# A four-layer encoder on one core: the layer norm's subtraction of the mean on VectorE instead of GpSimd

## The chip, the core and the metric

The kernel runs on one core of one Trainium2 chip. A core has five engines with a queue of instructions each: TensorE (PE: matmuls, and PEld, the weight loads), VectorE (DVE), ScalarE (ACT), GpSimd (POOL) and SyncE (SP, which issues most of the transfers here). An engine works through its queue in order; an instruction may wait for semaphores that other engines raise. The metric is the device time of one execution in microseconds (us), of which the median over several runs counts.

## What is computed

Sixteen meta tokens and 256 input tokens, 2048 wide, go through four layers. Each has an input projection, attention (neighbourhood attention in layers 1 and 4, differential attention in layer 2, a sliding window in layer 3), a gate, an output projection, and a layer norm of the scaled input plus the output. Cut to what matters here:

```python
def _layer_norm(x, g, b):
    xf = x.astype(F32)
    mu = jnp.mean(xf, -1, keepdims=True)
    var = jnp.mean(jnp.square(xf - mu), -1, keepdims=True)
    y = (xf - mu) * lax.rsqrt(var + LN_EPS) * g.astype(F32) + b.astype(F32)
    return y.astype(x.dtype)

for i in range(DEPTH):                       # 4 layers: kinds A, B, C, A
    y = branch_of_kind(h, w_in, ...)         # projection, attention, gate
    out = jnp.einsum('ble,ed->bld', y, w_out[i])
    h = _layer_norm(DEEPNORM_ALPHA * h + out, ln_g[i], ln_b[i])
```

## The kernel before

Activations lie transposed: the 2048 features as 16 tiles `d0` to `d15` of 128 partitions, the 272 tokens along the free axis. Every product is made of three matmuls in fp32r, with both operands split into a high and a low half: `mm3` issues high by high (L160), high by low (L161) and low by high (L162).

**Weights.** They arrive in chunks of 1 MB (`raw`, three buffers, issued on SP at L218). A chunk holds four granules; a granule is 128x512 weights, four k-tiles of one output tile, and feeds 12 matmuls. `split_to` splits each granule eight granules ahead of its use: ScalarE casts the high half `wh` (L168), VectorE subtracts it from `raw` to get the low half `wl` (L169). There are 9 buffers of each half. An output tile of a projection is 4 granules, 48 matmuls, collected in one of three PSUM banks `acc`.

**Between two layers.** When the last output tile of a layer is done, `norm_stats` sums over the features with four small matmuls (L795, L796) and VectorE and ScalarE make `negmu`, the negative mean (L802), and `rstd` (L803 to L809, where L809, kept as `self.newton`, is the last). In the meantime TensorE goes on: the first seven output tiles of the next layer (`deferred`) are multiplied with activations that have the factor g but neither mean nor deviation yet, called `h` or `y` in the rows. `rows` corrects their results afterwards: VectorE takes off the mean (L331), GpSimd multiplies by the deviation (L334, and L333 for the bias of a query tile).

**`normalise`** makes the true activations for the tiles from the eighth on. For each of the 16 tiles: GpSimd adds `negmu` to `d` (L825), VectorE multiplies by g and `rstd` (L827), ScalarE adds b and rounds to the high half (L830), VectorE makes the low half (L831). L827 may not stand ahead of L809 in VectorE's queue (`issue_after`); L825 has no such bound. This happens three times, ahead of layers 2, 3 and 4; the last norm has a function of its own, `norm_last`, in which VectorE does part of the additions (L848).

**What sets the order.** The four kinds of work (matmuls, splits, norm, attention tasks) are written in one program, and a scheduler orders the instructions of each engine when the kernel is built, by times that it estimates. The order is then fixed for the run.

In attention, `tr` are transposes (L484, L492, L629 to L631, L683), `sc` the scores, `nm` their row maxima (L533, L661), `vs` a value tile and `v_mid` a copy of its meta columns that GpSimd makes (L399, L401).

Of the kernel before, what the change touches and what calls it, by code (L numbers as in the profile page):

```python
# [14 lines left out]
ALU = mybir.AluOpType  # L15
# [89 lines left out]
def whole(t):  # L105
    return t.rearrange("p a b -> p (a b)")[:, :NTOK]
# [14 lines left out]
class Emit:  # L121
# [695 lines left out]
    def normalise(self, l):  # L817

        nc = self.nc
        negmu, rstd, _ = yield from self.need(("stats", l - 1), 0)  # L820
        self.nh, self.nl = [None] * KT, [None] * KT
        for k in range(KT):
            g, b = self.lnp[:, l - 1, k, 0:1], self.lnp[:, l - 1, k, 1:2]
            t = whole(self.d[k])
            nc.gpsimd.tensor_tensor(out=t, in0=t, in1=whole(negmu), op=ALU.add)  # L825
            with self.tc.issue_after(self.newton.ins):
                nc.vector.scalar_tensor_tensor(out=t, in0=t, scalar=g, in1=whole(rstd), op0=ALU.mult, op1=ALU.mult)  # L827
            yield
            self.nh[k], self.nl[k], _ = self.pair(l % 2, k)
            nc.scalar.activation(whole(self.nh[k]), t, AF.Identity, bias=b)  # L830
            nc.vector.scalar_tensor_tensor(out=whole(self.nl[k]), in0=t, scalar=b, in1=whole(self.nh[k]).bitcast(F32),  # L831
                                           op0=ALU.add, op1=ALU.subtract)
        self.done(("normalised", l))
# [172 lines left out]
```

## Time and profile before

| | |
|---|---|
| median of 3 runs | 1998.03 us (1996.39 to 1998.17) |
| profiled execution, its own time | 1996.35 us |
| its span, first to last instruction | 1994.5 us |
| TensorE busy | 1958.0 us, 98% of the span |
| VectorE busy | 1448.7 us, 73% |
| ScalarE busy | 1100.3 us, 55% |
| GpSimd busy | 495.8 us, 25% |
| granted TensorE clock, mean | 0.996 of full |

Busy time is a mean over the span. Whether an engine limits a stretch is read from that stretch: which engine has no gap there, and who waits for whom. The three norms between layers lie at about 540, 1075 and 1461 us after the span's start.

### The profile page before, as it was taken

To read this page: it belongs to the slowest core of one execution; us is meant where nothing else is said; L and a number is where in the kernel's file an instruction comes from. 1 tells how busy PE (TensorE), PEld (TensorE's weight loads), DVE (VectorE), ACT (ScalarE), POOL (GpSimd) and SP (SyncE) were. 2 spreads that over 40 slices of the span, in tenths; PEclk is the share of its full clock that TensorE was granted. 3 is DMA by queue.
4 is the path that set the end of the run, shared out by engine and by line. 5 is a ranking of instruction groups with operands and counts; after the bars stand their busy time and mean duration, and the time that the engine had idled before them with its cause. 6 is when DMAs were issued, how large, how long until landed. Compare 5 with 4: busy or idle time off the path is not lost.

```text
span 1994.5 us, 40444 instructions
## 1 busy us (share of the span) xinstructions
PE 1958.0 (98%) x15794; PEld 1948.4 (98%) x15794; DVE 1448.7 (73%) x2642; ACT 1100.3 (55%) x2381; POOL 495.8 (25%) x735
## 2 busy tenths in 40 slices
PE   9999999999999999999999999999999999999995
PEld 9999999999999999999999999999999999999995
DVE  6666666668798677767798987777988666666685
ACT  6555554554566555555555655565565555555553
POOL 1100011124443122112354332223542001110053
PEclk9999999999999999999999999999999999999998
DMA  8444444444454444444453444444435444444441
GB/s 277 170 162 166 167 160 169 156 164 154 154 185 149 150 168 149 162 162 149 149 188 128 170 148 149 149 152 174 169 128 202 160 173 175 166 168 174 168 174 61
DMA packets 53039, 323.97 MB, mean 162 GB/s; under 512 B 6256, under 2 KB 12528, under 8 KB 15344
## 3 DMA queue, kind: packets, MB, share of 16 engines
q1 hardware_dynamic: 51984, 320.76, 45.6%
q8 instruction: 124, 2.03, 0.4%
q10 hardware_dynamic: 864, 0.63, 0.1%
q14 instruction: 67, 0.55, 0.1%
HBM read 319.27 MB, written 2.10 MB: 161 GB/s over the span
## 4 chain that ended last, share of the span: by engine, by line
PE 92%; DVE 5%; issue 1%; DMA 1%; POOL 1%; ACT 0%; DVEq 0%; SPq 0%; ACTq 0%; POOLq 0%
PE acc L160 28%; PE acc L162 28%; PE acc L161 28%; DVE wl L169 2%; DVE d L827 1%; PE sc L162 1%; PE sc L161 1%; PE sc L160 1%; PE o L161 1%; PE o L162 1%; PE o L160 1%; PE tr L484 1%; PE tr L492 1%; POOL ht L334 0%; DMA raw<-in_wts 0%
## 5 line engine op out<-in xcount | busy, mean ns | idle before, releaser
L169 DVE TENSOR_TENSOR wl<-raw,wh 128x512 fp32r<-128x512 f32 x1184 | 865.8, 738 | 413.3 <-ACT wh L168 401.9
L168 ACT CAST wh<-raw 128x512 fp32r<-128x512 f32 x1184 | 724.0, 618 | 662.9 <-PE acc L161 631.6
L160 PE MATMUL acc<-y,wh 128*128 128x272 f32 (+2 forms) x2448 | 706.5, 289 | 0.0
L161 PE MATMUL acc<-y,wh 128*128 128x272 f32 (+2 forms) x2448 | 704.4, 288 | 0.0
L162 PE MATMUL acc<-y,wl 128*128 128x272 f32 (+2 forms) x2448 | 701.2, 286 | 2.1 <-DVE wl L169 2.1
L162 PE MATMUL acc<-h,wl 128*128 128x272 f32 (+3 forms) x2288 | 662.3, 290 | 4.9 <-DVE wl L169 4.7
L160 PE MATMUL acc<-h,wh 128*128 128x272 f32 (+3 forms) x2288 | 661.8, 290 | 1.4 <-ACT wh L168 1.3
L161 PE MATMUL acc<-h,wh 128*128 128x272 f32 (+3 forms) x2288 | 660.3, 289 | 0.0
L162 PEld LDWEIGHTS acc<-y,wl 128*128 128x128 f32 x2448 | 461.4, 188 | 3.3 <-DVE wl L169 3.2
L161 PEld LDWEIGHTS acc<-y,wh 128*128 128x128 f32 x2448 | 461.4, 188 | 0.0
L160 PEld LDWEIGHTS acc<-y,wh 128*128 128x128 f32 x2448 | 461.0, 188 | 0.4
L162 PEld LDWEIGHTS acc<-h,wl 128*128 128x128 f32 x2288 | 431.6, 189 | 7.8 <-DVE wl L169 7.5
L160 PEld LDWEIGHTS acc<-h,wh 128*128 128x128 f32 x2288 | 432.1, 189 | 2.3 <-ACT wh L168 1.9
L161 PEld LDWEIGHTS acc<-h,wh 128*128 128x128 f32 x2288 | 431.4, 189 | 0.0
L366 DVE RECIPROCAL ez<-ez 128x272 f32<-128x272 f32 (+1 forms) x64 | 116.8, 1825 | 25.3 <-POOL ez L364 25.3
L367 POOL TENSOR_TENSOR gate<-gate,ez 128x272 f32<-128x272 f32 (+1 forms) x64 | 65.6, 1026 | 112.3 <-DVE ez L366 112.2
L774 POOL TENSOR_TENSOR os<-os,d 128x272 f32<-128x272 f32 (+1 forms) x56 | 63.2, 1128 | 111.2 <-DVE d L724 69.8
L364 POOL TENSOR_SCALAR ez<-ez 128x272 f32<-128x272 f32 (+1 forms) x64 | 27.8, 434 | 197.6 <-ACT ez L363 197.4
L427 POOL MEMSET vs<- 128x16 f32 x32 | 3.6, 112 | 233.1 <-PE tr L492 194.6
L775 POOL TENSOR_TENSOR os<-os,sq 128x272 f32<-128x272 f32 (+1 forms) x56 | 54.5, 973 | 2.6 <-DVE wl L169 2.5
L825 POOL TENSOR_TENSOR d<-d,negmu 128x272 f32<-128x272 f32 x48 | 47.4, 1024 | 22.9 <-DVE negmu L802 22.9
L439 POOL MEMSET s<- 128x16 f32 x32 | 3.6, 113 | 174.0 <-PE tr L489 167.0
(271 smaller groups left out, 1915.9 us busy)
## 6 DMA issues: line engine op xcount, KB each, us to landing
raw<-in_wts SPq DMA_DIRECT2D x293, 1024.0 KB, 4.8
bias<-in_bias_a SPq DMA_DIRECT2D x32, 184.0 KB, 2.3
raw<-in_wts SPq DMA_DIRECT2D x12, 256.0 KB, 5.0
d<-in_xT SPq DMA_DIRECT2D x16, 136.0 KB, 4.5
out_h<-raw SPq DMA_DIRECT2D x8, 256.0 KB, 2.2
dist<-in_dist_b ACTq DMA_DIRECT2D x1, 272.0 KB, 5.2
dist<-in_dist_c ACTq DMA_DIRECT2D x1, 272.0 KB, 5.7
lnp<-in_lnp ACTq DMA_DIRECT2D x1, 64.0 KB, 2.6
```

Of the source, the lines that this page charges most:

```text
L160: mm(out, lhsT=lh, rhs=rh, start=start, stop=False)
L161: mm(out, lhsT=lh, rhs=rl, start=False, stop=False)
L162: mm(out, lhsT=ll, rhs=rh, start=False, stop=stop)
L168: nc.scalar.copy(out=hi, in_=src)
L169: nc.vector.tensor_sub(out=lo, in0=src, in1=hi.bitcast(F32))
L364: nc.gpsimd.tensor_scalar(out=view(ez), in0=view(ez), scalar1=1.0, scalar2=1.0, op0=ALU.mult, op1=ALU.add)
L366: nc.vector.reciprocal(view(ez), view(ez))
L367: nc.gpsimd.tensor_tensor(out=view(zc), in0=view(zc), in1=view(ez), op=ALU.mult)
L484: nc.tensor.transpose(tr[:96, at[c]:at[c] + 128], s[:, c // 2, c % 2 * 96:c % 2 * 96 + 96], ident)
L774: eng.tensor_tensor(out=view(self.s1), in0=view(self.s1), in1=d, op=ALU.add)
L775: eng.tensor_tensor(out=view(self.s2), in0=view(self.s2), in1=sq, op=ALU.add)
L825: nc.gpsimd.tensor_tensor(out=t, in0=t, in1=whole(negmu), op=ALU.add)
```

## The change

The 48 additions of `negmu` (16 at each of three norms) move from GpSimd to VectorE, and into the block that keeps them behind L809 in VectorE's queue. The operation, its operands and its results are the same. Everything else in the text is unchanged; the line of the addition becomes L826.

```diff
         for k in range(KT):
             g, b = self.lnp[:, l - 1, k, 0:1], self.lnp[:, l - 1, k, 1:2]
             t = whole(self.d[k])
-            nc.gpsimd.tensor_tensor(out=t, in0=t, in1=whole(negmu), op=ALU.add)
             with self.tc.issue_after(self.newton.ins):
+                nc.vector.tensor_tensor(out=t, in0=t, in1=whole(negmu), op=ALU.add)
                 nc.vector.scalar_tensor_tensor(out=t, in0=t, scalar=g, in1=whole(rstd), op0=ALU.mult, op1=ALU.mult)
             yield
             self.nh[k], self.nl[k], _ = self.pair(l % 2, k)
```

The built order changes with it. Counted by line and engine, nothing else is added or dropped. The places that differ lie in three stretches behind the three norms, of some 900, 740 and 590 rows of TensorE's queue; the rest stands as before. A `+` is a row of the changed kernel's queue, a `-` one of the kernel before, a row without either stands in both. The numbers behind a name tell buffers apart.

VectorE, at the first norm, from the end of the statistics on:

```order
 L808 SCALAR_TENSOR_TENSOR rst_1285_7077<-rsx_1284_7076,rst_1285_7077 128x272
 L809 SCALAR_TENSOR_TENSOR rstd_1282_7074<-rst_1285_7077,rstd_1282_7074 128x272
+L826 TENSOR_TENSOR d0_3_73<-d0_3_73,negmu_1281_7073 128x272
 L169 TENSOR_TENSOR wl_1287_7090<-raw_1243_6849,wh_1286_7089 128x512
+L826 TENSOR_TENSOR d1_4_74<-d1_4_74,negmu_1281_7073 128x272
 L169 TENSOR_TENSOR wl_1291_7112<-raw_1255_6926,wh_1290_7111 128x512
+L826 TENSOR_TENSOR d2_5_75<-d2_5_75,negmu_1281_7073 128x272
+L826 TENSOR_TENSOR d3_6_76<-d3_6_76,negmu_1281_7073 128x272
+L826 TENSOR_TENSOR d4_7_77<-d4_7_77,negmu_1281_7073 128x272
+L169 TENSOR_TENSOR wl_1295_7135<-raw_1255_6926,wh_1294_7134 128x512
```

The additions stand between the low halves of the weights: the third of these, `wl_1295`, has five of them in front, where three L827 stood before.

TensorE, in the third output tile behind the first norm (`acc_7273`); `acc_7362` and `acc_7449` are the fourth and the fifth:

```order
 L160 MATMUL acc_7273<-h_1188_6512,wh_7155 128x274
 L161 MATMUL acc_7273<-h_1188_6512,wh_7155 128x274
+L160 MATMUL acc_7362<-h_1136_6185,wh_7198 128x274
+L161 MATMUL acc_7362<-h_1136_6185,wh_7198 128x274
+L160 MATMUL acc_7449<-h_1136_6185,wh_7291 128x274
+L161 MATMUL acc_7449<-h_1136_6185,wh_7291 128x274
 L162 MATMUL acc_7273<-h_1188_6512,wl_7156 128x274
```

The first two matmuls of later tiles, which need a high half only, now stand ahead of a matmul that needs the low half `wl_7156`.

GpSimd, some 50 us behind the second norm, where `v_mid_2800` is the copy that the transpose L631 of the second value tile reads:

```order
 L334 TENSOR_TENSOR ht_2757_14860<-ht_2757_14860,rstdq_2667_14347 128x272
-L334 TENSOR_TENSOR ht_2774_14938<-ht_2774_14938,rstd_2666_14346 128x272
-L364 TENSOR_SCALAR ez_2791_15011<-ez_2791_15011 128x272
 L399 MEMSET v_mid_2800_15060 128x96
 L401 COPY v_mid_2800_15060<-vs_2786_15001 128x3x16
+L334 TENSOR_TENSOR ht_2774_14938<-ht_2774_14938,rstd_2666_14346 128x272
+L399 MEMSET v_mid_3038_16260 128x96
+L364 TENSOR_SCALAR ez_2791_15011<-ez_2791_15011 128x272
```

The copy moves ahead of a product (L334) and of a step of the gate (L364).

## Rows read from the trace of the kernel before

**Rows 1.** The page's first part: engine, busy us, share, instructions.

```profile
PE 1958.0 (98%) x15794; PEld 1948.4 (98%) x15794; DVE 1448.7 (73%) x2642; ACT 1100.3 (55%) x2381; POOL 495.8 (25%) x735
```

**Rows 2.** Stretches: from:to us, length, busy us by engine, clock, DMA share, GB/s.

```profile
16.00:540.00 524.00, 524.00 (x4234) 523.69 (x4234) 351.21 (x651) 276.44 (x590) 85.42 (x129) 1.00 0.49 174
540.00:600.00 60.00, 56.67 (x437) 55.21 (x436) 56.80 (x90) 39.62 (x87) 28.87 (x30) 1.00 0.45 158
```

**Rows 3.** TensorE's waits: what <- for whom: us in total, times, longest.

```profile
PE acc L162 <- DVE wl L169: 6.8, 15, 1.4
PE tr L631 <- POOL v_mid L401: 2.3, 1, 2.3
...
PE sc L160 <- DVE nm L533: 1.3, 1, 1.3
...
PE tr L484 <- DVE s L470: 0.7, 1, 0.7
```

**Rows 4.** TensorE's timeline: start us, us, what; in brackets idle time before it.

```profile
540.27 0.28 PE L160 MATMUL acc<-h,wh 128*128 128x274 f32 x1
...
544.85 0.29 PE L160 MATMUL acc<-h,wh 128*128 128x274 f32 x1
...
551.09 0.29 PE L161 MATMUL acc<-h,wh 128*128 128x274 f32 x1
551.49 0.39 PE L162 MATMUL acc<-h,wl 128*128 128x274 f32 x1
...
596.14 0.30 PE L160 MATMUL sc<-kh,qh 128*16 128x272 f32 x1 [1.29 <-DVE nm L533]
...
1074.68 0.29 PE L160 MATMUL acc<-y,wh 128*128 128x274 f32 x1
...
1123.83 0.28 PE L629 MATMUL tr<-ident,vs 128*128 128x128 f32 x1
...
1459.99 0.29 PE L160 MATMUL acc<-h,wh 128*128 128x260 f32 x1
...
1460.60 0.29 PE L162 MATMUL acc<-h,wl 128*128 128x260 f32 x1
...
1461.23 0.29 PE L160 MATMUL acc<-h,wh 128*128 128x260 f32 x1
...
1510.31 0.25 PE L160 MATMUL sc<-kh,qh 128*128 128x192 f32 x1
```

**Rows 5.** VectorE's timeline at the first norm: start us, us, what.

```profile
542.65 0.58 DVE L807 SCALAR_TENSOR_TENSOR rst<-rstd 128x272 f32<-128x272 f32 x1 [0.96 <-ACT rstd L806]
...
544.19 0.90 DVE L809 SCALAR_TENSOR_TENSOR rstd<-rst,rstd 128x272 f32<-128x272 f32 x1
545.02 2.44 DVE L169 TENSOR_TENSOR wl<-raw,wh 128x512 fp32r<-128x512 f32 x2
...
550.18 1.26 DVE L169 TENSOR_TENSOR wl<-raw,wh 128x512 fp32r<-128x512 f32 x1
551.36 1.00 DVE L827 SCALAR_TENSOR_TENSOR d<-d,lnp,rstd 128x272 f32<-128x272 f32 x1
...
557.69 0.49 DVE L827 SCALAR_TENSOR_TENSOR d<-d,lnp,rstd 128x272 f32<-128x272 f32 x1
558.10 0.68 DVE L169 TENSOR_TENSOR wl<-raw,wh 128x512 fp32r<-128x512 f32 x1
558.70 0.49 DVE L831 SCALAR_TENSOR_TENSOR y<-d,lnp,y 128x272 fp32r<-128x272 f32 x1
559.11 0.49 DVE L827 SCALAR_TENSOR_TENSOR d<-d,lnp,rstd 128x272 f32<-128x272 f32 x1
```

**Rows 6.** GpSimd's timeline at the first norm: sixteen additions in a row.

```profile
541.42 15.80 POOL L825 TENSOR_TENSOR d<-d,negmu 128x272 f32<-128x272 f32 x16 [7.75 <-DVE negmu L802]
```

**Rows 7.** A group by line and shape: count, busy us, mean ns, idle before.

```profile
L774 DVE TENSOR_TENSOR os<-os,d 128x272 f32<-128x272 f32 x3 | 1.3, 443 | 0.3
```

**Rows 8.** Weight transfers: issues, KB each, median us from issue to landing.

```profile
raw<-in_wts SPq DMA_DIRECT2D x293, 1024.0 KB, 4.8
```

## The prediction

> **What bounds the kernel now.** I read the engines' busy shares first. TensorE is busy 98% of the span [rows 1], so time can only be won where it stands still. The stretches show where: between 16 and 540 us it is busy 524.00 of 524 us, around the first norm 56.67 of 60 [rows 2]. Its waits say for whom: 6.8 us in 15 waits for the low halves of weights that VectorE makes, all but 0.2 of it behind the three norms, then 2.3 us once for a GpSimd copy and 1.3 us once for a score maximum [rows 3].
>
> These figures understate the loss, since the matmuls overlap in the rows. So I count places. Thirty-six matmuls of 274 columns take 544.85 - 540.27 = 4.58 us, 0.1273 each [rows 4]. At the first norm, 402 matmuls stand in the order between the one that starts at 540.27 and the score matmul at 596.14. At full pace that is 51.2 us and would end at 591.4: 4.7 us are lost, 1.3 of them in that score's own wait, so 3.4 to the low halves. At the second norm, 360 matmuls lie between 1074.68 and 1123.83: 45.8 us at full pace, 3.3 lost. At the third, 360 lie between 1461.23 and 1510.31; 192 of them have 256 or 260 columns, at 0.61/5 = 0.122 us [rows 4]: 192 x 0.122 + 168 x 0.1273 = 44.8, 4.3 lost. **Sum: 11.0 us** lost to late low halves, at three places.
>
> Why are they late? VectorE's timeline [rows 5] gives 1.2 us for one L169 and 1.00 for one L827 until 557, and from 557.69 on 0.49 and 0.68. GpSimd's sixteen additions run from 541.42 to 557.22 without a gap [rows 6]. Both engines slow down together: an addition takes 15.80/16 = 0.99 us, and VectorE's instructions with two operands in SBUF take about twice their time beside them. The chain L807 to L809, which nothing but the norm uses, is hit as well: 0.58, 0.90, 0.90 us. TensorE runs into it at 551.09: its next matmul needs the third low half behind L809, which ends at 551.44, and starts at 551.49 instead of 551.22 [rows 4, 5].
>
> **The change part by part.** *Removed:* 16 GpSimd additions per norm, 15.8 us of a queue that nobody waits for directly except L827. Their going is worth what they cost VectorE. From 542.65 to 557.69, 15.0 us, VectorE starts the last three statistics, six L169 and six L827. At the later pace, by starts, a 272-column instruction takes 0.41 us (558.70 to 559.11) and an L169 0.60 (558.10 to 558.70) [rows 5]: 9 x 0.41 + 6 x 0.60 = 7.3 us. So the additions cost VectorE 7.7 us per norm now.
>
> *Added:* 16 additions on VectorE. No such row of L826 exists; L774, the same shape and operands on VectorE, has 443 ns [rows 7], which I take as 0.41 from start to start like its neighbours. 16 x 0.41 = 6.6 us. Bounds: 0.41 with no one else on the port, 0.92 (1.00 less the overlap) if something still slows it. I take 0.41, since GpSimd has nothing else in its queue there until the L334 of the first corrected tile.
>
> So VectorE's load per norm is nearly the same: 7.7 off, 6.6 on. What decides is **when** the low halves come. I walk through VectorE's new order behind the first norm. L809 ends at 542.65 + 3 x 0.41 = 543.9, 1.1 us earlier than now. The third low half has five additions and two low halves in front: 5 x 0.41 + 3 x 0.60 = 3.85, done at 547.7; TensorE needs it at 551.2, and one more every 12 x 0.1273 = 1.53 us. The fourth has six more small instructions in front: 550.8 against 552.7. The tightest is the fourteenth: 14 x 0.60 + 35 x 0.41 = 22.75 us, at 566.7 against 551.2 + 11 x 1.53 = 568.0, early by 1.3 us. If L807 to L809 won nothing, it would still be early by 0.2. Behind it stand seven low halves with few small instructions between, and the lead grows to 5 us. The other two norms have the same order up to a few rows; at the third, tiles of 260 columns bring the need of the fourteenth forward by up to 0.6 us, and 0.7 remain. So TensorE's waits for low halves go: **-11.0 us**.
>
> *What is late next?* The additions push back the last activations: their low halves end, by the same sum, at 582.7. TensorE reads d15's at about the 375th matmul, 540.27 + 47.7 = 588.0: covered by 5 us. The corrected key tile that the first score reads comes about 4 us ahead of its place. ScalarE's casts follow L827 only through L830, and a cast needs a buffer that TensorE gives back; none of these comes later than its use by my sums, the closest by 1.1 us. A weight buffer is free when its last low half is made; that happens earlier, so SP issues earlier, and 4.8 us later [rows 8] the chunk is there. The last norm has its own additions and is untouched.
>
> *Moved:* the order of the attention that starts behind each norm. The two single waits of 2.3 and 1.3 us [rows 3] sit there. The copy for L631 moves ahead of the L334 that held it back, and the score matmuls stand further behind each other. Bounds: all 3.6 us gone, or as much again in new waits (-3.6 to +3.6). I take half the gain, **-1.8**, because the moves point that way, but a queue of some 740 moved rows has other places to wait.
>
> *Sum:* 1996.35 - 11.0 - 1.8 = 1983.6 for the profiled execution. The median of the runs lies 1.7 us above that execution, so I predict **1985.2 us**.
>
> **A rule against it.** In the 60 us around the norm VectorE is busy for 56.80, GpSimd for 28.87 [rows 2]. The Trainium skill's page "Perfetto Trace Analysis", section "Optimizing Scalar/DVE Operations", says that where VectorE is saturated, moving work to ScalarE or even GpSimd may make sense. By that, taking 16 additions back onto a full VectorE would cost 3 x 6.6 = 19.8 us. The same paragraph warns that the two share an SBUF read port and that moving work between them might not help; the rows side with the warning.
>
> **The rivals.** *Slower: the doubling has another cause.* If VectorE's long rows came from the weight transfers or from its own stream, the additions would come on top: at least 16 x 0.41 = 6.6 us per norm of a queue on which TensorE already waits, 19.8 in all, about 2018 us. It decides from the first low half behind L809: over 1.1 us there is this case. Against it: the rows change from 1.26 to 0.68 within half a microsecond of the last GpSimd addition, while the transfers go on. Chance 4%.
>
> *No change: the gain is given back.* The 11 us return as new waits in the moved stretches. In-order TensorE would have to stop, for instance, at the score matmul that now stands inside the eighth tile, some 42 us behind the sums, for a key tile that passes L331, L334 and L342. If each of the three such places waited for about 3.5 us, the time would be 1994 to 1998. For it: the order was made for estimated times, and the present waits show that they can miss by 2 us. Against it: by my sums each operand has 1 to 5 us to spare. Chance 14%. A miss of that kind by more ends slower: 2%.
>
> *Half the gain.* The fourteenth low half and its neighbours come 1 to 2 us late because VectorE's steps are 0.44 and not 0.41, and the waits halve: 1990 us. Chance 20%, inside the range.
>
> *More.* Both single waits go, and the next in the list, 0.7 us for attention weights behind the third norm [rows 3]: 1998.03 - 11.0 - 3.6 - 0.7 = 1982.7, and up to 2 us less with the smallest. Chance 15%.
>
> **How the numbers follow.** Forecast (1983 to 1988) 45%, half the gain 20%, more 15%, no change 14%, slower 6%. The range reaches from a little under "more" to the edge of "no change": 1980.0 to 1994.5. A measurement here can tell about 0.2%, 4 us, from no change: faster (under 1994.0) 0.80, same 0.14, slower 0.06.
>
> **What would show it.** Right: L169 and L827 rows of 0.68 and 0.49 right behind L809; L807 to L809 within 1.3 us; the wait of L162 for L169 near zero in the list of waits; TensorE busy about 59 of 60 us from 540 to 600; GpSimd at 448 us. Wrong: low halves of over 1 us without a GpSimd row beside them, or a new line in TensorE's waits (for kh, y, wh or an acc bank) that is larger than 3 us.

## The result and the profile after

| | before | after |
|---|---|---|
| median of the runs | 1997.21 us (1995.77 to 1998.17, 4 runs) | 1980.3 us (1978.7 to 1981.21, 4 runs) |
| span of the profiled execution | 1994.5 us | 1976.9 us |
| TensorE, VectorE, GpSimd busy | 1958.0, 1448.7, 495.8 us | 1952.9, 1443.8, 461.0 us |

The ratio of the times is 0.9915, with a 95% interval of 0.9903 to 0.9927: 16.9 us faster. The forecast was 12.8 us (1985.2 from 1998.03); the measured time lies inside the range, 0.3 us above its lower edge of 1980.0. Measured a second time (`after_again`, beside e3 below) the changed kernel took 1978.48 us (1978.41 to 1978.8) against 1997.08, 18.6 us faster and just below the range. Between the profiled executions of the table the gain is 1994.5 - 1976.9 = 17.6 us.

The page's first part of the changed kernel, to be held against [rows 1]:

```profile
PE 1952.9 (99%) x15794; PEld 1948.9 (99%) x15794; DVE 1443.8 (73%) x2690; ACT 1100.3 (56%) x2381; POOL 461.0 (23%) x687
```

VectorE has 48 instructions more than before and is busy 4.9 us **less**. That can only be if its other instructions became shorter. The stretches around the three norms (from:to, length, busy us of PE, PEld, DVE, ACT, POOL, clock, DMA share, GB/s), to be held against the second row of [rows 2]:

```profile
540.00:600.00 60.00, 60.00 (x476) 59.92 (x475) 56.49 (x115) 42.08 (x92) 15.89 (x13) 1.00 0.48 167
1070.00:1140.00 70.00, 70.00 (x565) 69.91 (x564) 67.72 (x147) 49.27 (x114) 20.83 (x26) 1.00 0.48 167
1456.00:1520.00 64.00, 64.00 (x522) 64.00 (x521) 62.39 (x128) 43.15 (x99) 15.93 (x15) 1.00 0.56 205
```

TensorE has no gap behind any norm any more: 476 matmuls stand in the first 60 us, where 437 stood before. Its complete list of waits:

```profile
PE acc L160 <- ACT wh L168: 1.3, 2, 0.8
PE o L257 <- DVE ones L254: 1.0, 1, 1.0
PE tr L308 <- DVE lamp L303: 0.6, 1, 0.6
```

All three lie at the start of the program. The waits for `wl`, `v_mid`, `nm` and `s` of [rows 3] are gone, and no new one came. VectorE's timeline at the first norm (start us, us, what), to be held against [rows 5]:

```profile
542.62 0.44 DVE L807 SCALAR_TENSOR_TENSOR rst<-rstd 128x272 f32<-128x272 f32 x1 [0.96 <-ACT rstd L806]
...
543.58 0.44 DVE L809 SCALAR_TENSOR_TENSOR rstd<-rst,rstd 128x272 f32<-128x272 f32 x1
543.94 0.43 DVE L826 TENSOR_TENSOR d<-d,negmu 128x272 f32<-128x272 f32 x1
544.29 0.69 DVE L169 TENSOR_TENSOR wl<-raw,wh 128x512 fp32r<-128x512 f32 x1
...
546.90 0.69 DVE L169 TENSOR_TENSOR wl<-raw,wh 128x512 fp32r<-128x512 f32 x1
...
548.91 0.50 DVE L827 SCALAR_TENSOR_TENSOR d<-d,lnp,rstd 128x272 f32<-128x272 f32 x1
```

L809 took 0.90 us and takes 0.44, L827 1.00 and now 0.50, L169 1.26 and now 0.69. The third low half starts at 546.90 and is done at 547.59.

**Where the 17.6 us are.** The statistic L802, once per norm, cuts the span into layers. Before, then after:

```profile
540.90 0.44 DVE L802 TENSOR_SCALAR negmu<-sc 128x272 f32<-128x272 f32 x1 [1.17 <-ACT rst L801]
...
1075.31 0.44 DVE L802 TENSOR_SCALAR negmu<-sc 128x272 f32<-128x272 f32 x1 [1.11 <-ACT rst L801]
...
1461.87 0.44 DVE L802 TENSOR_SCALAR negmu<-sc 128x272 f32<-128x272 f32 x1 [1.00 <-ACT rst L801]
...
1973.26 0.42 DVE L802 TENSOR_SCALAR negmu<-sc 128x256 f32<-128x256 f32 x1 [1.23 <-ACT rst L801]
```

```profile
540.87 0.44 DVE L802 TENSOR_SCALAR negmu<-sc 128x272 f32<-128x272 f32 x1 [1.17 <-ACT rst L801]
...
1071.27 0.44 DVE L802 TENSOR_SCALAR negmu<-sc 128x272 f32<-128x272 f32 x1 [1.09 <-ACT rst L801]
...
1450.01 0.44 DVE L802 TENSOR_SCALAR negmu<-sc 128x272 f32<-128x272 f32 x1 [1.00 <-ACT rst L801]
...
1956.01 0.42 DVE L802 TENSOR_SCALAR negmu<-sc 128x256 f32<-128x256 f32 x1 [1.23 <-ACT rst L801]
```

The same subtraction for the kernels below gives this table (us from norm to norm; in brackets the difference to the kernel before; t16_11 and t16_16 have the three numbers of the second profile):

| kernel | layer 2 | layer 3 | layer 4 |
|---|---|---|---|
| before | 534.41 | 386.56 | 511.39 |
| after | 530.40 (-4.0) | 378.74 (-7.8) | 506.00 (-5.4) |
| after, second profile | 529.48 (-4.9) | 378.74 (-7.8) | 506.00 (-5.4) |
| e1, GpSimd adds beside it | 534.51 (+0.1) | 384.70 (-1.9) | 510.85 (-0.5) |
| e2, GpSimd fills zeros | 529.61 (-4.8) | 378.74 (-7.8) | 507.82 (-3.6) |
| e2b, GpSimd copies | 530.64 (-3.8) | 380.98 (-5.6) | 506.91 (-4.5) |
| e4, first norm only | 529.48 (-4.9) | 386.49 (-0.1) | 511.39 (0.0) |
| e5, old order, small additions | 530.11 (-4.3) | 379.02 (-7.5) | 505.81 (-5.6) |
| e3, no additions | 529.21 (-5.2) | 378.89 (-7.7) | 505.81 (-5.6) |

The three gains of the changed kernel make 17.2 us, in its second profile 18.1; before the first norm and behind the last one nothing over 0.4 us changed from the kernel before to the first profile. The 0.9 us between the two profiles of one kernel were lost far behind the norm: from 1000 to 1072 us the first has 574 matmuls and the second 580; why stays open. Where the additions are out of the way, a layer differs by up to 2 us from kernel to kernel (505.81 to 507.82 in layer 4, for which e2 below has a reason); smaller differences are not read from the table.

### The profile page after: what moved, and what is told of

Same layout as the page of the kernel before. It is cut to its first block, busy times and chain, and to the rows that moved or that the text cites. A ratio compares the mean times of both kernels' runs of the same rounds, so it can differ in the third digit from the quotient of the medians.

```text
span 1976.9 us, 40433 instructions
## 1 busy us (share of the span) xinstructions
PE 1952.9 (99%) x15794; PEld 1948.9 (99%) x15794; DVE 1443.8 (73%) x2690; ACT 1100.3 (56%) x2381; POOL 461.0 (23%) x687
## 4 chain that ended last, share of the span: by engine, by line
PE 98%; DVE 1%; DMA 1%; ACT 0%; issue 0%; SPq 0%; DVEq 0%
PE acc L160 30%; PE acc L162 30%; PE acc L161 30%; PE sc L162 1%; PE sc L161 1%; PE sc L160 1%; PE o L161 1%; PE o L162 1%; PE o L160 1%; PE tr L492 1%; PE tr L484 1%; DMA raw<-in_wts 0%; PE tr L683 0%; DVE d L850 0%; DVE d L848 0%; DMA dist<-in_dist_b 0%
## 5 line engine op out<-in xcount | busy, mean ns | idle before, releaser
L169 DVE TENSOR_TENSOR wl<-raw,wh 128x512 fp32r<-128x512 f32 x1184 | 857.7, 732 | 403.4 <-ACT wh L168 393.3
L168 ACT CAST wh<-raw 128x512 fp32r<-128x512 f32 x1184 | 725.1, 619 | 675.0 <-PE acc L161 649.8
L364 POOL TENSOR_SCALAR ez<-ez 128x272 f32<-128x272 f32 (+1 forms) x64 | 28.5, 445 | 193.8 <-ACT ez L363 193.7
L160 PE MATMUL sc<-kh,qh 128*128 128x272 f32 (+2 forms) x176 | 45.2, 259 | 0.0
L161 PE MATMUL sc<-kl,qh 128*128 128x272 f32 (+2 forms) x176 | 44.4, 257 | 0.0
```

The source lines that it names most:

```text
L160: mm(out, lhsT=lh, rhs=rh, start=start, stop=False)
L161: mm(out, lhsT=lh, rhs=rl, start=False, stop=False)
L168: nc.scalar.copy(out=hi, in_=src)
L169: nc.vector.tensor_sub(out=lo, in0=src, in1=hi.bitcast(F32))
L364: nc.gpsimd.tensor_scalar(out=view(ez), in0=view(ez), scalar1=1.0, scalar2=1.0, op0=ALU.mult, op1=ALU.add)
```

## The experiments

The theory: GpSimd's additions hold up VectorE's instructions with two operands in SBUF (the memory on the core that the engines work on), VectorE falls behind, and TensorE waits. The rivals: it was the additions' place behind L809, or the new order of the queues.

**e1: GpSimd adds again, for nothing.** The changed kernel with this behind `t = whole(self.d[k])`, where `spare` are two scratch tiles:

```diff
+            nc.gpsimd.tensor_tensor(out=spare[k % 2], in0=whole(negmu), in1=whole(negmu), op=ALU.add)
```

> The changed kernel, and beside each of the 48 additions that VectorE now does GpSimd makes one of the same size whose result nobody reads (it adds negmu to negmu into two scratch tiles). The order on TensorE, VectorE and ScalarE is that of the changed kernel, row by row; only GpSimd's queue has 16 rows more at each norm. Contention (my theory): while GpSimd adds, some 16 us per norm, VectorE's rows with two operands in SBUF double again (L169 1.2 us, L826 and L827 0.9 to 1.0, L807 0.58), VectorE falls some 8 us behind, the tightest low half, which comes 2.0 us early in the changed kernel, comes 6 us late: L162 <- L169 is back at the head of TensorE's waits and the time is 1980.3 + 3 x 6 = 1998 us (1994 to 2003). Rival, that the gain came from the additions' place behind L809 and from the new order of the queues: L169 stays near 0.7 us and the time near 1980 (1978 to 1983).

Measured: 1995.06 us (1994.4 to 1996.46), 0.9991 of the kernel before (0.9981 to 1.0). Beside GpSimd's 48 idle additions nearly the whole gain is gone. GpSimd's (L826) and VectorE's rows (L828 is the addition here) at the first norm, and the first line of TensorE's waits:

```profile
543.94 0.64 POOL L826 TENSOR_TENSOR sumh<-negmu 128x272 f32<-128x272 f32 x1 [7.82 <-DVE negmu L802]
...
548.39 1.08 POOL L826 TENSOR_TENSOR sumh<-negmu 128x272 f32<-128x272 f32 x1
549.44 0.84 POOL L826 TENSOR_TENSOR suml<-negmu 128x272 f32<-128x272 f32 x1
```

```profile
547.86 1.12 DVE L169 TENSOR_TENSOR wl<-raw,wh 128x512 fp32r<-128x512 f32 x1
548.90 0.87 DVE L828 TENSOR_TENSOR d<-d,negmu 128x272 f32<-128x272 f32 x1
...
557.73 0.43 DVE L828 TENSOR_TENSOR d<-d,negmu 128x272 f32<-128x272 f32 x1
```

```profile
PE acc L162 <- DVE wl L169: 8.6, 7, 2.6
```

The addition takes 0.87 us beside GpSimd and 0.43 at 557.73, where GpSimd has done its last one; the wait for low halves is back. Since no row of TensorE's, VectorE's or ScalarE's queue moved, this is **contention; with the new place and order still there, 2.2 us of the gain are left** (1997.26 - 1995.06, hardly clear of no change). The loss is 14.8 us against 18 expected. For one thing, these additions read one operand twice and hold VectorE up by less than the old ones did (below). For another, the waits for `v_mid`, `nm` and `s` did not come back with those for low halves; e5 returns to that.

**e2: GpSimd just as busy, but reading nothing.** The same, with

```diff
+            for i in range(3):
+                nc.gpsimd.memset(spare[i % 2], 0.0)
```

> The same, but GpSimd fills the scratch tiles with zeros, three times for each addition (3 x 16 x 0.33 = 15.8 us per norm, the length of the sixteen additions): it writes and reads nothing. Contention for reads: L169 stays at 0.7 us, L826 at 0.44, time 1980 (1978 to 1983). Contention of any GpSimd access: as with the additions, about 1998. Third possibility, that GpSimd's being busy costs by itself, since its products L334 and copies L401 start up to 16 us later: VectorE's rows short, but TensorE waits for v_mid or for a key tile behind the norms, 1983 to 1990; this would say that part of the gain was GpSimd's queue coming free.

Measured: 1980.58 us (1980.1 to 1980.98), 0.9921 (0.9904 to 0.9937), the time of the changed kernel. GpSimd's stream, and VectorE beside it:

```profile
551.49 5.69 POOL L827 MEMSET sumh<- 128x272 f32 x15
```

```profile
551.67 0.69 DVE L169 TENSOR_TENSOR wl<-raw,wh 128x512 fp32r<-128x512 f32 x1
```

L169 stays at 0.69, and a fill takes the expected 0.33 us beside it (15 in 5.69 us, with short pauses). GpSimd's queue coming free earlier is no part of the gain that can be seen: with some 13 us of fills in front of its products per norm the time is the same. One wait is new, 1.4 us at the third norm for a high half that ScalarE made late (L168); it makes most of the 1.8 us by which layer 4 is longer. ScalarE had itself waited 5.6 us for a product of GpSimd that took 7.43 us, some 15 us behind the last fill (last section).

**e2b: one operand read.**

```diff
+            nc.gpsimd.tensor_copy(spare[k % 2], whole(negmu))
```

> The same, but GpSimd copies negmu into the scratch tiles, once for each addition (16 x 0.62 = 10 us per norm): one operand read, one written. If only GpSimd's instructions with two operands are in VectorE's way: L169 0.7 us beside them, time 1980 (1978 to 1983). If any read is: VectorE's rows double for 10 us, it falls 5 us behind, the tightest low half comes 3 us late, 1980.3 + 3 x 3 = 1989 (1985 to 1993).

Measured: 1984.05 us (1983.54 to 1984.76), 0.9938 (0.9923 to 0.9953): between the two cases. VectorE (L828 is the addition) beside the copies and a microsecond behind their first half:

```profile
546.27 0.64 DVE L828 TENSOR_TENSOR d<-d,negmu 128x272 f32<-128x272 f32 x1
546.83 0.89 DVE L169 TENSOR_TENSOR wl<-raw,wh 128x512 fp32r<-128x512 f32 x1
547.65 0.43 DVE L828 TENSOR_TENSOR d<-d,negmu 128x272 f32<-128x272 f32 x1
548.00 0.68 DVE L169 TENSOR_TENSOR wl<-raw,wh 128x512 fp32r<-128x512 f32 x1
```

A read of one operand holds VectorE up too, by half as much: L169 0.89 us. So "VectorE doubles" was wrong in general; what the expectation took from it, 5 us behind per norm and 1989 us, came out 5 us too slow, and the other case, no effect up to 1983, 1 us too fast. By e1, e2 and e2b it is GpSimd's **reads** that count. The Trainium skill's page "SBUF — State Buffer", section "Who interferes with whom", says the same: a VectorE instruction with two SBUF inputs contends with a GpSimd instruction that reads SBUF, and not with one that only writes. The trace agrees: L169 takes 0.69 us beside the fills, 0.89 beside the copies and 1.12 beside the additions of e1.

**e4: the first norm only.** In `normalise` the addition is VectorE's for `l == 1` and GpSimd's for `l > 1`.

> The change at the first norm only; the second and third keep GpSimd's additions. If each norm's gain is its own (my theory): from negmu to negmu (L802) layer 2 takes 530.4 us as in the changed kernel, layers 3 and 4 386.6 and 511.4 as before, and the time is 1997.2 - 4.0 = 1993.2 us (1992 to 1995). If the gain of layer 3, 7.8 us and more than the 3.3 us counted for its low halves, is owed to what layer 2 leaves behind: 1990 or less.

Measured: 1991.6 us (1990.8 to 1992.81), 0.9973 (0.9964 to 0.9983), 1.6 us below the expectation and 0.4 below its range. Layers 3 and 4 are as before to 0.1 us (table above), so each norm's gain is its own. Layer 2 gives 4.9 us, 0.9 more than in the first profile of the changed kernel, from which the expectation was made, and as much as in its second (529.48 both). In its list of waits those of layers 3 and 4 still stand, and `nm`, which was layer 2's, is gone:

```profile
PE acc L162 <- DVE wl L169: 4.8, 11, 1.4
PE tr L631 <- POOL v_mid L401: 2.3, 1, 2.3
```

**e5: no contention in the old order.** The kernel before, with

```diff
-            nc.gpsimd.tensor_tensor(out=t, in0=t, in1=whole(negmu), op=ALU.add)
+            nc.gpsimd.tensor_tensor(out=t[:, :8], in0=t[:, :8], in1=whole(negmu)[:, :8], op=ALU.add)
```

> The kernel before, with GpSimd's 48 additions cut to 8 of the 272 columns (the mean is taken off these columns only). GpSimd is nearly silent at the norms, VectorE gets nothing added, and the order is that of the kernel before: in layers 2 and 3 TensorE's queue differs in six rows (L162) behind each norm only, GpSimd's in the place of one L334. So this is the contention alone, without the moved attention. If the gain has two parts (my theory): the waits for low halves go, 11 us, and the other waits of the kernel before stay where the order stayed, v_mid 2.3 us and nm 1.3 us in the list of waits: 1997.1 - 11.0 = 1986 us (1984 to 1988). Rival, that those waits too were VectorE's lateness: they go as well and the time is that of the changed kernel, 1979 to 1981.

Measured: 1978.99 us (1978.72 to 1979.76), 0.991 (0.9893 to 0.9926): the rival's forecast, 1979 to 1981, was right. The waits for `v_mid` and `nm` are gone although in layers 2 and 3 the attention has its old order on TensorE and GpSimd: **a lighter VectorE is enough to remove them.** GpSimd's queue at the second norm shows why. The second value tile itself was ready early in the kernel before (ScalarE's last step on it, L342, ends at 1114.97), but the copy of its meta columns (L401), which the transpose L631 waits for, stands behind a product for the gate (L334), and that waits for VectorE's L331. Before, then e5:

```profile
1124.22 0.49 DVE L331 SCALAR_TENSOR_TENSOR ht<-negmu,ht 128x272 f32<-128x272 f32 x1
...
1124.79 2.17 POOL L334 TENSOR_TENSOR ht<-ht,rstd 128x272 f32<-128x272 f32 x1 [2.00 <-DVE ht L331]
...
1129.21 0.22 POOL L401 COPY v_mid<-vs 128x48 f32<-128x48 f32 x1
```

```profile
1112.36 0.49 DVE L331 SCALAR_TENSOR_TENSOR ht<-negmu,ht 128x272 f32<-128x272 f32 x1
...
1112.92 2.17 POOL L334 TENSOR_TENSOR ht<-ht,rstd 128x272 f32<-128x272 f32 x1 [2.60 <-DVE ht L331]
...
1117.35 0.22 POOL L401 COPY v_mid<-vs 128x48 f32<-128x48 f32 x1
```

Counted from L802 (1075.31 and, in e5, 1070.91), L331 stands at 48.9 us before and at 41.4 in e5: 7.5 us earlier, nearly the 7.7 us that the additions cost VectorE. (VectorE's rows stand in another order in e5, but the same 75 of them lie between.) The copy moves from 53.9 to 46.4. So in the kernel before the single wait of 2.3 us hung on the same backlog, carried over 50 us by VectorE's queue to GpSimd and from there to TensorE.

It does not follow that the moved order did nothing. In e1 the order is the new one and VectorE is late again, and the copy, TensorE's L631 and VectorE's L331 come like this:

```profile
1126.91 0.61 POOL L401 COPY v_mid<-vs 128x48 f32<-128x48 f32 x1
...
1129.55 0.27 PE L631 MATMUL tr<-ident,v_mid 128*96 128x128 f32 x1
...
1130.41 0.48 DVE L331 SCALAR_TENSOR_TENSOR ht<-negmu,ht 128x272 f32<-128x272 f32 x1
```

L331 stands 52.5 us behind L802 (1077.86), later than in the kernel before, and yet the copy is made at 49.0, ahead of it, and TensorE does not wait. **So the moved order alone is enough, too.** The changed kernel has both: its L331 stands at 46.6 us, 2.4 earlier than before, its copy at 45.0, 8.9 earlier.

**e3: the price of the additions on VectorE.** The changed kernel with the line of L826 left out.

> The changed kernel without the 48 additions, on any engine: the mean is not taken off the sixteen activation tiles at the three norms. It gives the price of the additions on VectorE. If TensorE's own work is all that is left behind the norms (my theory): nothing to win, the time of the changed kernel within 1 us. Rival, that VectorE's 16 x 0.41 = 6.6 us per norm still stand on the path: up to 3 x 2.0 = 6 us less where they use up the lead of the tightest low half, 1974; by the rule that VectorE is the saturated engine, 3 x 6.6 = 19.8 us less, 1960.

Beside it the changed kernel ran once more:

> The changed kernel once more, as the measure for the three kernels run beside it: 1980.3 us as before (1978.5 to 1981.5).

Measured: 1978.86 us (1978.16 to 1979.31) without the additions, 1978.48 (1978.41 to 1978.8) with them. Without the additions TensorE's queue was built as in e5, in the old order of the attention, so the two kernels differ in more than the additions. Neither has a wait of TensorE's behind a norm: TensorE's own work is all that is left there, and there VectorE's 48 additions cost nothing that can be measured.

**t16_11 and t16_16: the last norm too.** The tail behind the last L802 is where TensorE has no work left and VectorE and GpSimd still share the additions and products of `norm_last`.

```diff
-TAIL = (8, 10, 11)
+TAIL = (16, 16, 11)     # t16_11; (16, 16, 16) in t16_16
```

> The changed kernel, and the same change at the last norm: all sixteen additions (L848) and products (L850) on VectorE, none on GpSimd (TAIL = 16, 16, 11). Until then every queue is as in the changed kernel. Contention: VectorE's 0.86 us from start to start in the tail become 0.34, so 3 + 32 + 5 instructions x 0.34 = 13.6 us from 1956.7 to 1970.3, against 1972.8 now: 2.5 us less than the changed kernel, 1977.8 (1977 to 1979). If the tail's rows are long for another reason, the 14 instructions taken from GpSimd come on top: 14 x 0.86 = 12 us more at most, 1980 to 1992.

> As the one before, and ScalarE makes all sixteen last steps (L852), VectorE none of L854 (TAIL = 16, 16, 16). Contention: 3 + 32 instructions x 0.34 = 11.9 us, VectorE ends at 1968.6, ScalarE's last row 0.6 later, 3.6 us before the 1972.8 of now: 1976.7 (1975.5 to 1978). If ScalarE's sixteen rows of 0.52 set the end, no better than the one before.

Measured beside the changed kernel's 1978.48 us: t16_11 1975.33 us (1974.31 to 1976.84), t16_16 **1974.29 us** (1973.95 to 1974.86), 0.9886 of the kernel before (0.9871 to 0.9901). Three products in a row in the tail and the last ones, in the changed kernel and then in t16_16:

```profile
1961.69 2.68 DVE L850 TENSOR_TENSOR d<-d,rstd 128x256 f32<-128x256 f32 x3
...
1971.13 0.41 DVE L850 TENSOR_TENSOR d<-d,rstd 128x256 f32<-128x256 f32 x1
```

```profile
1958.82 1.09 DVE L850 TENSOR_TENSOR d<-d,rstd 128x256 f32<-128x256 f32 x3
...
1967.20 1.09 DVE L850 TENSOR_TENSOR d<-d,rstd 128x256 f32<-128x256 f32 x3
```

Alone, VectorE starts one every 0.33 us and has done all 32 additions and products at 1968.29; beside GpSimd, which takes 14 of them, one product takes 0.87 from start to start and its own share lasts until 1971.54, from nearly the same start (L802 at 1955.53 and 1956.01). It is the same effect at a fourth place, with 3.2 us won where 2.5 were expected (t16_11) and 4.2 where 3.6 were (t16_16). Both times lie below their expected ranges, which were counted from 1980.3 us and not from the 1978.48 beside them. By the medians t16_16 is the fastest kernel of the study.

## Why the prediction was right, point by point

The time fell into the range by 0.3 us, and the second measurement would have missed it by 1.5. The mechanism was right; one term of the sum was too small by about 4 us, and that the range held in spite of it is in part luck.

- **The bound** (right). What could be won lay behind the three norms, and it is won there: 4.0 (4.9 in the second profile), 7.8 and 5.4 us.
- **The cause** (right, shown by e1 and e2). The last GpSimd addition and VectorE's jump from 1.26 to 0.68 us at 557.7 were cause and effect.
- **VectorE's new walk** (right). Forecast and measured: third low half 547.7 and 547.59, fourteenth 566.7 and 566.04, L807 to L809 within 1.3 us by starts (542.62 to 543.94), L826 0.41 from start to start and in fact 0.35. The walk took the clean pace for all of it, however, and that failed at its end: the corrections' products (L334) on GpSimd contend from 571 us on, and the last low half of the activations came at 585.3, not 582.7. Half of the 5 us of cover was used up. What helped against it was the step of 0.35: the 16 additions cost VectorE 5.6 us and not 6.6. GpSimd is busy 461 us and not 448; these products are not why (1 us less in sum than before), the rest is spread over many lines and was not followed up.
- **The low halves, -11.0 us by places** (right). In the changed kernel the same counts of places in TensorE's queue, 402, 360 and 360, take 51.05, 45.47 and 44.90 us (540.25 to 591.30, 1070.64 to 1116.11, 1449.38 to 1494.28) where they took 55.87, 49.15 and 49.08: 12.7 us less, and 11.4 without the score's own wait of 1.3. The sum of the wait rows, 6.8 us, would have missed 4.
- **The moved stretches, -1.8 us** (the term that was mis-sized). Measured were 17.2 - 11.4 = 5.8 us, 6.7 by the second profile. I priced only the first two single waits, 3.6 us, and halved them for new waits that never came. But all seven waits behind the norms went. Beside the three of [rows 3], 4.3 us, these four of the kernel before, 1.2 us:

```profile
PE tr L683 <- DVE pm L385: 0.5, 1, 0.5
PE sc L161 <- DVE kl L352: 0.3, 1, 0.3
PE tr L685 <- POOL s_mid L678: 0.2, 1, 0.2
PE tr L683 <- DVE s L673: 0.2, 1, 0.2
```

  The sum should have been 11.0 + 5.5 = 16.5, which gives 1998.03 - 16.5 = 1981.5 us. The reason given, that the copy moves ahead of the L334 that held it back, was sound: in e1, where VectorE is late again, none of the seven is in the list of waits (a new one of 0.4 us, for `s_mid`, is). What the prediction did not see is the second way: by e5 those of layers 2 and 3 also leave in the old order once VectorE is lighter. In layer 4 e5 moved TensorE's scores and transposes as well, so there it does not tell the two apart. How the two share the gain in the changed kernel, where VectorE is 7.7 - 5.6 = 2.1 us lighter per norm, stays open.
- **The rule weighed** (the rows were right). The forecast by the rule was 19.8 us lost; measured were 16.9 won, and e3, with its other order, puts the price of the additions at less than 1 us. The paragraph weighed, in the Trainium skill's page "Perfetto Trace Analysis", section "Optimizing Scalar/DVE Operations", says that a saturated VectorE may give work away, and warns that moving work between VectorE and GpSimd might not help; the warning is what happened here.
- **The rivals.** "More" (15%) was nearest, with its 1982.7 us and up to 2 less. "Slower" is refuted by the time and by e1, "no change" and "half the gain" by the empty list of waits: the fourteenth low half came 2 us early.

## What to carry to other kernels

A GpSimd instruction that reads SBUF beside a dense stream of VectorE instructions with two SBUF operands was paid twice here, once on each engine; work that GpSimd seems to take off VectorE for free can cost VectorE more than doing it (7.7 us against 16 x 0.35 = 5.6 here). Look for rows of the same line and shape with two durations, and at what the other engine does at the moment of the jump. And where one engine is late, price every later wait that its queue feeds, even 50 us on and through another engine, not only the waits that name it.

## What the runs showed that was not expected

**The price is per GpSimd instruction.** In e1 GpSimd's additions start 0.80 us apart beside L828 and 1.05 apart beside an L169 (548.39 to 549.44), exactly as VectorE's instructions do: the two go through one by one. Start to start, L828 grows from 0.35 to 0.80 us and L169 from 0.60 to 1.04, both by 0.45; beside the copies of e2b both grow by 0.21 to 0.22 (546.27 to 546.83, 546.83 to 547.65), beside the old additions, which read two different tiles, L827 and L169 take 0.51 and 0.58 longer (1.00 against 0.49, 1.26 against 0.68) [rows 5]. So sixteen additions cost VectorE sixteen times about half a microsecond, whichever of these instructions it runs meanwhile.

**A lone GpSimd instruction loses.** Two rows of GpSimd in the changed kernel, and one of e2:

```profile
548.95 2.10 POOL L333 TENSOR_SCALAR ht<-ht 128x1 f32<-128x1 f32 x1 [15.31 <-ACT ht L327]
...
588.20 4.17 POOL L334 TENSOR_TENSOR ht<-ht,rstd 128x272 f32<-128x272 f32 x1 [4.70 <-DVE ht L331]
...
1481.00 7.43 POOL L334 TENSOR_TENSOR ht<-ht,rstdq 128x256 f32<-128x256 f32 x1 [2.03 <-DVE ht L331]
```

One element per partition takes 2.10 us (0.29 in the next such row, at 556.87), and a product that takes 0.97 at 575.81 takes 4.17, while VectorE keeps its clean pace beside them (four L169 in 2.49 us from 588.04). In e2 such a product took 7.43 us, 3.99 at the same place in the changed kernel, and TensorE paid 1.4 us for it. Why a stream of GpSimd instructions gets every second turn and a single one has to wait was not tried.

**A long wait can cost clock as well.** In e1 TensorE waits 2.64 us in one piece, until 558.81. The stretches around it show the granted clock falling behind that wait from 1.00 to 0.58 of full, most of the time at the lower level of 1.2 GHz, and coming back:

```profile
556.00:558.00 2.00, 0.17 (x2) 0.00 (x0) 2.00 (x4) 0.17 (x1) 1.50 (x2) 1.00 0.00 0
...
560.00:562.00 2.00, 2.00 (x12) 2.00 (x11) 2.00 (x5) 1.51 (x4) 0.00 (x0) 0.58 0.84 201
562.00:564.00 2.00, 2.00 (x12) 2.00 (x11) 2.00 (x6) 1.87 (x5) 0.04 (x1) 0.57 0.77 324
564.00:566.00 2.00, 2.00 (x18) 2.00 (x17) 2.00 (x6) 1.18 (x3) 0.53 (x1) 1.00 0.00 0
```

Twelve matmuls fall into 2 us instead of 18. In layer 2 of e1 the wait of 2.6 us and about 1.7 us of lost clock (0.42 and 0.43 of 2 us each) make 4.3 us; it is slower than the two profiles of the changed kernel by 4.1 and 5.0. At the third norm the same comes behind a wait of 2.65 us (0.63 and 0.52 from 1478 to 1482); behind the waits at the second norm, 2.26 us the longest, the clock stays at 1.00.
